# Changing the accumulator layout two blocks ahead of the attention projection, and opening that projection's first two pairs together

## The chip, the cores and the metric

The kernel runs on one core of one Trainium2 chip. The metric is the time of one launch on the device, in microseconds (us); lower is better. The profile shows one execution, engine by engine: TensorE (PE, with its weight loads as PEld), VectorE (DVE), ScalarE (ACT), GpSimd (POOL) and SyncE (SP), the last of which only issues DMAs here.

## The reference

One layer of a decoder, for a prompt of 1024 tokens and 8 single-token samples, 1032 columns in all. Three mixers read the same normalised input; each one's output is projected, multiplied by its gate and summed, and the sum goes through the merge weights:

```python
D_MODEL = 1024; ATTN_HEADS = 4; SSM_D_INNER = 2048; MEM_LEN = 256
sc_b, sc_c, sc_x, z, xbc, dt_raw, q, gates = jnp.split(xn @ w_in, splits, axis=-1)
y_a = (sc_b * conv_u) @ w_sc_out                                  # short convolution
y_b = group_rmsnorm(y_ssd, ssm_norm_w, SSM_GROUPS) @ w_ssm_out    # state-space scan
...                                                               # attention into 256 memory tokens
y_c = attention @ w_attn_o
x = x + (g_a * y_a + g_b * y_b + g_c * y_c) @ w_merge_o
x = x + swiglu(rmsnorm(x))
```

The change touches the end of `y_b`'s projection, all of `y_c`'s, and the sum of the three gated shares. (The last five lines above are shortened from the reference's `mixer_block` and its caller.)

## The kernel before, in words

Activations lie with features on the 128 partitions and the 1032 columns along the free axis. Every f32 matrix product is three products of rounded halves: each operand is split into a high part `h` (a rounding copy on ACT) and a low part `l` (a subtraction on DVE), and PE multiplies high by high, high by low and low by high into one accumulator. A weight block of 1024 rows and 128 columns is loaded by SP into a "raw" tile and split.

PSUM, the accumulators' memory, has 8 banks. Up to the point of the change it is laid out as two accumulators of three banks (`mm_ps`; function `gemm` writes one for each output block, in pieces of 260, 512 and 260 columns, while the other is evicted) and two small ones. Then `mm_stack.close()` drops these, and the pool `pst` lays out three accumulators of two banks, `m0`, `m1`, `m2`, each for half of the columns (`HT` = 516).

The stretch around the change runs as follows.

- `out_part(2, m, ...)` computes the last eight output blocks of `y_b`, in accumulators `po20` to `po27`. For each it loads a gate (`gt`) and the part summed so far (`yr`), adds the accumulator to `yr` on DVE (L1497), multiplies by the gate (L1498), and leaves the store to `yg_d` to be issued during the next block (`owed`). So `yg_d` holds the gated share of `y_b`, and `mg_d` that of `y_a`.
- The attention for the samples runs beside these blocks (`so`, `os_d`, `psob`: their outputs, stored, loaded in another layout and transposed).
- `y_c` is computed with one level of a Strassen-like scheme, by pairs of output blocks: `ao0`, `ao2`, `ao4`, `ao6`. The columns of the activations are split in halves, and sums and differences of their quarters, called forms (`B11`, `B21`, `T1`, `nT2`, `T3`, `B22`, `T4`), are multiplied by a pair's weights (`A`), sums of them (`S`, `T`) or a part of them (`D`): seven products of 24 matmuls, 168 a pair. Each form and each weight combination is split in halves by ACT and DVE. `st_begin` loads and prepares the first pair. `strassen` runs a pair: `B11`, `T1`, `nT2`, `B21`, `T3`, `B22`, `T4`, with evictions on ACT and DVE (L381 subtracts the accumulator of `T3`, L383 that of `B22`) between them.
- In `fetch`, in the middle of each pair, SP loads the gate `gt` and `yg`, and POOL issues a DMA that adds `mg_d` onto `yg`. When the pair is done DVE multiplies by the gate and adds `yg` (L1859 to L1865), which gives two blocks of the sum, the tiles `mg0` to `mg7`.
- These are split (`mgs0h`, `mgs0l`, ...) and multiplied by the merge weights (`wm00` and so on) into accumulators `pm`.

Each engine runs its instructions in the order that a scheduler fixed when the program was built; each of SP's and POOL's DMAs waits in its queue until what it needs is there. Tiles come from pools that rotate (weights three of each kind, `ev` five), so an allocation waits for the last reader of the oldest tile.

Of the kernel before, what the change touches and what calls it, by code (L numbers as in the profile page):

```python
# [17 lines left out]
P = 128  # L18
# [25 lines left out]
def tile_kernel(ctx: ExitStack, tc, a, o):  # L44
# [8 lines left out]

    cp = ctx.enter_context(tc.tile_pool(name="const", bufs=1))
    wp = ctx.enter_context(tc.tile_pool(name="weights", bufs=3))
    ap_ = ctx.enter_context(tc.tile_pool(name="acts", bufs=12))
# [32 lines left out]
    V.memset(ones, 1.0)  # L89
    tri = cp.tile([P, P], F32, tag="tri", name="tri")  # L90
    G.affine_select(
# [107 lines left out]
    def gemm(w, acts, name, width=P, off=0):  # L199
# [19 lines left out]
        return ps  # L219

    def wblock(w, col):
        return w[:, col : col + P].rearrange("(k p) c -> p k c", p=P)
# [7 lines left out]
    freed = [None]  # L230
    count = [0]

# [39 lines left out]
    def st_early(blocks, forms):  # L272


        for first in range(0, len(blocks), 3):
            held = []
            for i, (src1, nm, out, keep) in enumerate(blocks[first : first + 3]):
                wA = st_split(st_raw(src1, f"{nm}Er"), f"{nm}E")
                ps = st_ps(f"m{i}", f"{nm}e")
# [36 lines left out]

    def strassen(src1, src2, forms, nm, sums, outs, early=None, after_t3=None, ready=None, hook=None, add=False, begun=None, mid=None):

# [3 lines left out]
        elif ready is None and early is None:  # L322
            raw1, raw2 = st_raw(src1, f"{nm}r1"), st_raw(src2, f"{nm}r2")
        tags = ("m0", "m1", "m2") if count[0] % 2 == 0 else ("m2", "m1", "m0")
        count[0] += 1
        pa, pb = (st_ps(t, f"{nm}{t}") for t in tags[:2])

# [10 lines left out]
        if early is None:  # L338
            pc = st_ps(tags[2], f"{nm}{tags[2]}")
            if begun is None:  # L340
                wA = st_split(raw1, f"{nm}A")
            prod(pa, wA, 0, "B11", True)
        else:
            tick()
        if ready is not None:
            raw1, raw2, sa, wS, wT = ready
        elif early is not None:
            raw1, raw2, sa, wS = st_sums(src1, src2, nm, sums, freed[0])
        else:
            if begun is None:  # L350
                sa = sums(f"{nm}sa")
                V.tensor_add(sa[:, :512], raw2[:, :512], raw2[:, 512:])
                V.tensor_add(sa[:, 512:], sa[:, :512], raw1[:, :512])
                wS = st_split(sa, f"{nm}S")
            put(o11, pa)
        if ready is None:
# [8 lines left out]
        if early is None:  # L365
            put(o12, pa)
            prod(pc, wA, 512, "B21", True)
            V.tensor_tensor(o11, hv(pc), o11, op=ALU.add)
# [52 lines left out]

    tail_sc = cp.tile([P, 1, 10, 8], F32, tag="tail_sc", name="tail_sc")
    tail_xc = cp.tile([P, 3, 11, 8], F32, tag="tail_xc", name="tail_xc")
    qs = cp.tile([P, 8, NS], F32, tag="qs", name="qs")

# [1048 lines left out]
    def out_part(i, m, w, src, nxt):  # L1474


        nm = f"{i}{m}"
        if m == 0:
            out_in(src)
        if i != 1:  # L1480
            gt = ev_tile(f"gt{nm}")
            SY.dma_start(gt[:, :TT], gt_d[(0, 8, 8)[i] + m])
        if i == 2:
            t = ev_tile(f"yr{nm}")
            SY.dma_start(t[:, :TT], yr_d[m])
        if m == KD - 1 and nxt is not None:
            out_ahead(nxt)
        ps = gemm(weights(wblock(w, m * P), f"wo{nm}"), acts, f"po{nm}")
        if i == 0:
            V.tensor_mul(gt[:, :TT], flat(ps), gt[:, :TT])  # L1490
            owed.append(lambda: SY.dma_start(mg_d[m], gt[:, :TT]))
        elif i == 1:
            t = ev_tile(f"yr{nm}")
            S.copy(t[:, :TT], flat(ps))
            S.dma_start(yr_d[m], t[:, :TT])
        else:
            V.tensor_tensor(t[:, :TT], flat(ps), t[:, :TT], op=ALU.add)  # L1497
# [3 lines left out]
    split = []  # L1501
    outs = deque()
    ins = ((sc_d, a["w_sc_out"][0]), (yb_d, a["w_ssm_out"][0, 0:D]), (yb_d[8:16], a["w_ssm_out"][0, D : 2 * D]), (None, None))
# [72 lines left out]
    if True:  # L1576
# [228 lines left out]
        ats_stack.close()  # L1805
        assert not pend
        while len(outs) > 1:
            run_next(outs)
        for c in (slice(0, T - HT), slice(T - HT, HT)):
# [15 lines left out]
    pst_stack = ExitStack()  # L1825
    pst[0] = pst_stack.enter_context(tc.tile_pool(name="pst", bufs=1, space=PSUM))
    ev_sums = lambda n: ev_tile(n, (P, 1024))
    wa = [wblock(a["w_attn_o"][0], m * P) for m in range(KD)]
    begun = st_begin(wa[0], wa[1], "ao0", ev_sums)
    for kt in range(4):  # L1830
        b12, b22 = raw8[kt][:, HS[1]], raw8[kt + 4][:, HS[1]]
        V.tensor_sub(b12, b22, b12)
        aform("T3", kt, b12)
    for kt in range(4):
        aform("B22", kt, raw8[kt + 4][:, HS[1]])
    for kt in range(4):
        t2, b21 = raw8[kt][:, HS[0]], raw8[kt + 4][:, HS[0]]
        V.scalar_tensor_tensor(t2, t2, -1.0, b21, op0=ALU.mult, op1=ALU.subtract)
        aform("T4", kt, t2)

    merged = []
    for m in range(0, KD, 2):
        oo = [ev_tile(f"ao{m}{i}")[:, :TT] if m == 0 else big(f"mg{m + i}") for i in range(2)]
        gts, ygs = [], []

        def fetch():
            for i in range(2):
                gts.append(ev_tile(f"gt3{m + i}")[:, :TT])
                SY.dma_start(gts[i], gt_d[16 + m + i])
                ygs.append(ev_tile(f"yg{m + i}")[:, :TT])  # L1850
                SY.dma_start(ygs[i], yg_d[m + i])
# [6 lines left out]
        merged += oo if m else [big(f"mg{i}") for i in range(2)]  # L1858
# [3 lines left out]
        V.tensor_mul(oo[1][:, c1], oo[1][:, c1], gts[1][:, c1])  # L1862
        V.tensor_add(merged[m + 1][:, c1], oo[1][:, c1], ygs[1][:, c1])
        V.scalar_tensor_tensor(oo[1][:, c0], pa, -1.0, gts[1][:, c0], op0=ALU.mult, op1=ALU.mult)
        V.tensor_add(merged[m + 1][:, c0], oo[1][:, c0], ygs[1][:, c0])  # L1865
    fxo_stack.close()
# [6 lines left out]
    mg = [split_act(merged[m], f"mgs{m}") for m in range(KD)]  # L1873
    turn_ = deque(("m0", "m1", "m2") if count[0] % 2 else ("m2", "m1", "m0"))

# [40 lines left out]
    for half in range(2):  # L1916
        sq = ev_tile(f"sq{half}")
        for m in range(KD):
# [26 lines left out]
            else:  # L1945
                ps = st_ps(turn_[0], f"pm{half}{m}")
                turn_.rotate(-1)
                merge_part([hv(ps)[:, lo:hi] for lo, hi in HALF], (0, 1))
# [170 lines left out]
    for part, js in enumerate(([0], [9, 10])):  # L2119
# [7 lines left out]

        tags = ("m0", "m1", "m2") if count[0] % 2 == 0 else ("m2", "m1", "m0")
        puts = []
        for m in range(KD):  # L2130
            if not part:
                x2[m] = big(f"x3_{m}")
            for half in range(2):
                ps = st_ps(tags[(2 * m + half) % 3], f"pd{part}{m}{half}")
                for k, (ah, al) in enumerate(hl):
# [10 lines left out]
                else:  # L2146
                    puts.append(S.copy(t, hv(ps)).ins)
        count[0] += 1

        with nullcontext() if part else tc.issue_after(puts[3]):  # L2150
# [178 lines left out]
```

## Time and profile before

| what | value |
|---|---|
| runs, median of 3 | 2444.56 us (2442.44 to 2445.43) |
| profiled execution, its own time | 2446.0 us |
| its span | 2444.3 us |
| mean granted clock of TensorE | 0.996 |
| PE busy | 2394.4 us, 98% |
| DVE, ACT, POOL busy | 67%, 46%, 5% |
| the stretch of the change | about 1529 us (end of `po25`) to 1654 us (first `pm`) |

A row of the timeline reads: start, duration, engine, line, operation, output<-inputs, count, and in brackets the idle time before it and what ended that. The granted clock is the share of full speed that TensorE was allowed.

### The profile page before, as it was taken

Reading aid. Unit: us, or ns where it says so; the run is one execution under the profiler, and the core shown is the slowest. Engines: PE = TensorE matmul, PEld = TensorE weight load, DVE = VectorE, ACT = ScalarE, POOL = GpSimd, SP = SyncE. Lnnn points to the kernel's source line nnn. Section 1 sums busy time; section 2 is a strip of 40 time slices with the busy share of each in tenths; the row PEclk is TensorE's granted clock in tenths of the full one; section 3 lists DMA queues with packets and bytes.
Section 4 is the critical chain, followed back from the end, with each engine's and each line's share of the span. In section 5 each row is a group of like instructions: output and inputs, shape, how many; then the busy total and the mean of one; then the engine's idle time right before and its main releaser. Section 6 shows DMA issues by size and latency. Waiting matters only on the chain.

```text
span 2444.3 us, 45555 instructions
## 1 busy us (share of the span) xinstructions
PE 2394.4 (98%) x18812; PEld 2283.4 (93%) x18812; DVE 1647.5 (67%) x2688; ACT 1112.7 (46%) x1792; POOL 111.5 (5%) x171
## 2 busy tenths in 40 slices
PE   8999999999999999999999999899999999999998
PEld 7999999999999999888888887899999999999998
DVE  6744686777777775568687763764777655567865
ACT  6634555455454544657555442333543333343423
POOL 0000000000000000212211000000000000000000
PEclk9999999999999999999999999999999999999999
DMA  6444423444454346679796887575455332354622
GB/s 213 133 157 155 130 91 111 129 139 130 130 152 118 113 122 194 200 225 296 240 295 213 270 309 271 172 205 182 141 179 163 105 106 95 101 182 149 190 86 80
DMA packets 356678, 407.90 MB, mean 167 GB/s; under 512 B 15230, under 2 KB 276462, under 8 KB 356463
## 3 DMA queue, kind: packets, MB, share of 16 engines
q1 hardware_dynamic: 332182, 337.50, 45.0%
q10 hardware_dynamic: 23137, 63.26, 6.8%
q0 software_dynamic: 1152, 4.23, 0.9%
q8 instruction: 148, 2.42, 0.4%
q14 instruction: 59, 0.48, 0.1%
HBM read 288.81 MB, written 116.35 MB: 166 GB/s over the span
## 4 chain that ended last, share of the span: by engine, by line
PE 84%; DMA 6%; DVE 6%; ACT 1%; issue 1%; SPq 0%; DVEq 0%; ACTq 0%; POOLq 0%; POOL 0%
PE po L218 8%; PE pm L1934 4%; PE ps_q L218 3%; PE py L1063 1%; PE pss L1076 1%; PE ps_z L218 1%; DMA yg<-mg_d 1%; PE po L1055 1%; PE G16m L267 1%; PE d00m L267 1%; PE Z2m L267 1%; PE Z14m L267 1%; PE X18m L267 1%; PE Z10m L267 1%; PE Z6m L267 1%
## 5 line engine op out<-in xcount | busy, mean ns | idle before, releaser
L1007 ACT ACTIVATE r<-r,acum 128x128 f32<-128x128 f32 x256 | 79.3, 391 | 2.9 <-DMA r<-ac_d 2.1
L796 DVE SCALAR_TENSOR_TENSOR ax<-u,prm,ax 128x1024 f32<-128x1024 f32 x44 | 56.3, 1280 | 0.0
L948 ACT ACTIVATE st<-st,es 128x128 f32<-128x128 f32 x128 | 41.3, 392 | 22.4 <-DMA st<-in_state_ssm_dram 22.4
L1040 POOL TENSOR_TENSOR xdd<-xdt,decst 128x512 f32<-128x512 f32 x32 | 35.3, 1102 | 284.3 <-DVE xdt L1036 275.9
L1034 DVE TENSOR_TENSOR r<-r,cbm 128x1024 f32<-128x1024 f32 x32 | 39.1, 1223 | 4.3 <-ACT r L1009 2.4
L1059 DVE TENSOR_TENSOR y<-po,ea 128x512 f32<-128x512 f32 x28 | 19.3, 690 | 31.7 <-PE po L1055 31.7
L950 DVE SCALAR_TENSOR_TENSOR st<-sr,dts,st 128x128 f32<-128x128 f32 x128 | 40.3, 346 | 0.4
L1076 PE MATMUL pss<-xdd,bT 128*128 128x512 f32 x64 | 34.5, 620 | 2.2 <-ACT bT L1033 1.7
L954 DVE SCALAR_TENSOR_TENSOR sr<-st,sr 128x128 f32<-128x128 f32 x128 | 35.4, 286 | 1.1
L1063 PE MATMUL py<-r,xdt 128*64 128x128 f32 x512 | 35.0, 279 | 0.0
L1009 ACT ACTIVATE r<-r 128x1024 f32<-128x1024 f32 x32 | 33.8, 1058 | 0.7
L1949 DVE TENSOR_TENSOR x<-pm,xT 128x516 f32<-128x516 f32 x15 | 10.4, 694 | 34.1 <-PE pm L1934 34.1
L1089 POOL TENSOR_TENSOR s<-s,cdec 128x512 f32<-128x512 f32 x28 | 33.1, 1182 | 0.9 <-DVE s L1082 0.7
L1063 PEld LDWEIGHTS py<-r,xdt 128*64 128x64 f32 x512 | 27.3, 136 | 4.4 <-issue 1.0
L1055 PE MATMUL po<-bc,s 128*128 128x128 f32 x224 | 29.6, 275 | 0.0
L1055 PEld LDWEIGHTS po<-bc,s 128*128 128x128 f32 x224 | 28.0, 191 | 1.0
L1627 ACT ACTIVATE pr<-psa,mx 128x256 f32<-128x256 f32 x32 | 14.9, 471 | 30.2 <-DVE mx L1625 30.2
L799 DVE SCALAR_TENSOR_TENSOR ax<-u,prm,ax 128x1032 f32<-128x1032 f32 x22 | 28.3, 1286 | 0.0
L793 ACT ACTIVATE ax<-u,prm 128x1024 f32<-128x1024 f32 x22 | 27.4, 1246 | 1.7 <-DVE u L383 0.4
L1615 DVE SCALAR_TENSOR_TENSOR kc<-kc,qb 128x256 f32<-128x256 f32 x64 | 23.8, 419 | 5.6 <-DMA qb<-qs_d 5.4
L1036 DVE TENSOR_TENSOR xdt<-xp,dtT 128x512 f32<-128x512 f32 x32 | 21.9, 684 | 8.0 <-PE xp L1029 8.0
L1033 ACT COPY bT<-bp 128x128 f32<-128x128 f32 x32 | 8.4, 262 | 38.5 <-DVE cbm L1031 38.5
(9290 smaller groups left out, 9046.0 us busy)
## 6 DMA issues: line engine op xcount, KB each, us to landing
r<-ac_d SPq DMA_DIRECT2D x32, 512.0 KB
gt_d<-G ACTq DMA_DIRECT2D x24, 516.0 KB
gt<-gt_d SPq DMA_DIRECT2D x24, 516.0 KB
xs_d<-ax ACTq DMA_DIRECT2D x22, 516.0 KB
zs<-zs_d SPq DMA_DIRECT2D x16, 516.0 KB
yb_d<-x SPq DMA_DIRECT2D x16, 516.0 KB
in<-yb_d SPq DMA_DIRECT2D x16, 516.0 KB
st<-in_state_ssm_dram SPq DMA_DIRECT2D x32, 256.0 KB
```

What stands on the lines that cost most here:

```text
L218: PE.matmul(po, wt[:, ks], xc, start=(k == 0 and i == 0), stop=(k == nk - 1 and i == 2))
L267: PE.matmul(po, wt[:, ks], xc, start=(start and kt == 0 and i == 0), stop=(kt == 3 and i == 2), skip_group_check=True,)
L796: V.scalar_tensor_tensor(acc[:, :T], u[:, j : j + T], w[j], acc[:, :T], op0=ALU.mult, op1=ALU.add)
L948: S.activation(st[:, i], st[:, i], AF.Copy, scale=es[:, g * 4 + i, b : b + 1])
L950: V.scalar_tensor_tensor(st[:, i], rb, dts[:, g * 4 + i, b : b + 1], st[:, i], op0=ALU.mult, op1=ALU.add)
L954: V.scalar_tensor_tensor(rb, st[:, i], 1.0, rc, op0=ALU.mult, op1=ALU.mult, accum_out=ys[:, g * 4 + i, b : b + 1],)
L1007: S.activation(r[:, j, :], r[:, j, :], AF.Relu, scale=-1.0, bias=acum[:, c, h : h + 1])
L1034: V.tensor_tensor(r, r, bc(cbm.unsqueeze(1), [P, HPG, P]), op=ALU.mult)
L1055: PE.matmul(po[:, t * P : (t + 1) * P], state["s"][:, t * P : (t + 1) * P], bcg[1][:, cs], start=True, stop=True,)
L1063: PE.matmul(py[hp : hp + 64, (h // 2) * P : (h // 2 + 1) * P], xdt[:, h * 64 : (h + 1) * 64], r[:, (h % 2) * 4 + h // 2, :], start=True, s ...
L1076: PE.matmul(pss, bT, xdd, start=True, stop=True)
L1934: PE.matmul(po, wt[:, ks], x[:, half * HT + lo : half * HT + hi], start=(k == 0 and i == 0), stop=(k == KD - 1 and i == 2),)
```

## The change

The last two output blocks of `y_b` are computed in the new layout by a new function `gemm_halves`: block 26 first for one half of the columns, then for the other, each in an accumulator of two banks; block 27 with both halves side by side. The layout is changed ahead of block 26. The three accumulators rotate by a list, `accs`, in place of the counter `count`.

The projection's first two pairs open together: `st_head` computes `B11` and `B21` of `ao0` and then of `ao2`, before the other products of either; `st_begin` of `ao0` moves ahead of block 27, and the forms of `T3`, `B22` and `T4` are made inside `ao0` (`hook`, `after_t3`). For these two pairs DVE only multiplies by the gate, into the tiles `mg0` to `mg3`, and POOL's DMAs add `yg_d` and `mg_d` onto them, two for each tile. Pairs `ao4` and `ao6` add their shares as before. Some small constants move into a pool (`cx`) that is closed ahead of this, and four gate tiles come from the pool `fxo`.

```diff
+    def gemm_halves(w, acts, name, put, joint):
+        n = int(pace[0] + pace[1])
+        pace[1] += pace[0] - n
+        parts = ((0, 1),) if joint else ((0,), (1,))
...
+        for part in parts:
+            pss = [next_ps(f"{name}{h}") for h in part]
+            for k, (ah, al) in enumerate(acts):
...
+                for i, (wt, x) in enumerate(((w[0], ah), (w[0], al), (w[1], ah))):
+                    for h, ps in zip(part, pss):
+                        for po, xc in halves_of(ps, x, h * HT):
+                            PE.matmul(
...
+            for h, ps in zip(part, pss):
+                put(hv(ps), HS[h])
...
+    def st_head(wA, forms, nm, o11, tags):
+        pa, pc = (st_ps(t, f"{nm}{t}") for t in tags)
+        st_prod(forms, pa, wA, 0, "B11", True)
+        S.copy(o11, hv(pa))
+        st_prod(forms, pc, wA, 512, "B21", True)
+        V.tensor_tensor(o11, hv(pc), o11, op=ALU.add)
+        return pa
+
+    def next_ps(name):
+        ps = st_ps(accs[0], name)
+        accs.rotate(-1)
+        return ps
...
-        ps = gemm(weights(wblock(w, m * P), f"wo{nm}"), acts, f"po{nm}")
+        wm = weights(wblock(w, m * P), f"wo{nm}")
+        if i == 2 and m >= KD - 2:
+            if m == KD - 2:
+                mm_stack.close()
+                pst[0] = pst_stack.enter_context(tc.tile_pool(name="pst", bufs=1, space=PSUM))
+
+            def put(ps, c):
+                V.tensor_tensor(t[:, c], ps, t[:, c], op=ALU.add)
+                V.tensor_mul(t[:, c], t[:, c], gt[:, c])
+
+            gemm_halves(wm, acts, f"po{nm}", put, m == KD - 1)
+            owed.append(lambda: SY.dma_start(yg_d[m], t[:, :TT]))
+            return
+        ps = gemm(wm, acts, f"po{nm}")
...
+        begun = st_begin(wa[0], wa[1], "ao0", ev_sums)
         for c in (slice(0, T - HT), slice(T - HT, HT)):
...
-    mm_stack.close()
...
+    raw_b = st_raw(wa[2], "ao2r1")
+    ta, tb, tc_ = accs
+    heads_ = [st_head(begun[3], aforms, "ao0", oos[0][0][:, HS[0]], (ta, tb))]
+    wA2 = st_split(raw_b, "ao2A")
+    heads_.append(st_head(wA2, aforms, "ao2", oos[1][0][:, HS[0]], (tc_, tb)))
...
+            for i in range(2 if m >= 4 else 0):
                 ygs.append(ev_tile(f"yg{m + i}")[:, :TT])
                 SY.dma_start(ygs[i], yg_d[m + i])
                 G.dma_start(ygs[i], mg_d[m + i], accum_op=ALU.add)
...
-            begun=begun if m == 0 else None, mid=fetch,
+            begun=begun if m < 4 else None, mid=fetch, hook=None if m else form3,
+            after_t3=None if m else last_aforms, head=heads_[m // 2] if m < 4 else None,
...
-        V.tensor_mul(oo[0], oo[0], gts[0])
-        V.tensor_add(merged[m], oo[0], ygs[0])
...
+        V.tensor_mul(merged[m], oo[0], gts[0])
+        V.tensor_mul(merged[m + 1][:, c1], oo[1][:, c1], gts[1][:, c1])
+        if m >= 4:
+            V.tensor_add(merged[m], merged[m], ygs[0])
+            V.tensor_add(merged[m + 1][:, c1], merged[m + 1][:, c1], ygs[1][:, c1])
+        V.scalar_tensor_tensor(merged[m + 1][:, c0], pa, -1.0, gts[1][:, c0], op0=ALU.mult, op1=ALU.mult)
+        if m >= 4:
+            V.tensor_add(merged[m + 1][:, c0], merged[m + 1][:, c0], ygs[1][:, c0])
+        else:
+            for src in (yg_d, mg_d):
+                for i in range(2):
+                    G.dma_start(merged[m + i], src[m + i], accum_op=ALU.add)
```

Three places show what this does to the order of instructions. The first is PE at the end of block 26 (`po_16905` before, `po_16964` its second half after; `ao0m` are accumulators of pair ao0). Before:

```order
10571 L218 MATMUL po_16905<-b07h,wo26l 128x512
10572 L218 MATMUL po_16905<-b07h,wo26l 128x260
10573 L218 MATMUL po_17065<-b00h,wo27h 128x260
10574 L218 MATMUL po_17065<-b00h,wo27h 128x512
10575 L218 MATMUL po_17065<-b00h,wo27h 128x260
```

And now:

```order
10596 L242 MATMUL po_16964<-b07h,wo26l 128x260
10597 L295 MATMUL ao0m_17227<-aB110ah,ao0Ah 128x256
10598 L1744 MATMUL psob<-ident,osr 128x8 x8
10599 L295 MATMUL ao0m_17227<-aB110ah,ao0Ah 128x260
...
10621 L295 MATMUL ao0m_17227<-aB112ah,ao0Al 128x260
10622 L242 MATMUL po_17115<-b00h,wo27h 128x256
```

The 24 matmuls of ao0's `B11` moved ahead of block 27. By the rotation of `accs`, `ao0m_17227` is the accumulator `m1`, which the second half of block 26, `po_16964`, held before it.

The second place is DVE in pair ao2, where L381 of before is L429 now (`ao4r` and `ao4sa`, `ao4sb`, `ao4Al` are the next pair's raw weights, sums and low part). Before:

```order
1603 L352 TENSOR_TENSOR ao4sa<-ao4r_17641 128x512
1604 L353 TENSOR_TENSOR ao4sa<-ao4sa,ao4r_17639 128x512
1605 L255 TENSOR_TENSOR ao2Dl<-ao2r_17420,ao2Dh 128x512
1606 L368 TENSOR_TENSOR mg_17416<-ao2m_17424,mg_17416 128x516
1607 L255 TENSOR_TENSOR ao4Al<-ao4r_17639,ao4Ah 128x1024
1608 L381 TENSOR_TENSOR mg_17417<-mg_17417,ao2m_17422 128x516
```

And now:

```order
1604 L398 TENSOR_TENSOR ao4sa<-ao4r_17690 128x512
1605 L283 TENSOR_TENSOR ao4Al<-ao4r_17688,ao4Ah 128x1024
1606 L399 TENSOR_TENSOR ao4sa<-ao4sa,ao4r_17688 128x512
1607 L327 TENSOR_TENSOR ao4sb<-ao4r_17688,ao4r_17690 128x512
1608 L328 SCALAR_TENSOR_TENSOR ao4sb<-ao4sa,ao4r_17688 128x512
1609 L429 TENSOR_TENSOR mg_17528<-mg_17528,ao2m_17283 128x516
```

Both steps of `ao4sb` moved ahead of the subtraction of `T3`, which stands behind the first use of `ao4r` in either order.

The third place is POOL's queue from the end of the scan on (`mg_17519` and `mg_17520` are mg0 and mg1, `mg_17678` and `mg_17528` mg2 and mg3, `yg_17813` to `yg_18037` yg4 to yg7). Before, it held the eight additions of `mg_d` to yg0 to yg7. Now:

```order
166 L1952 DMA mg_17519<-yg_d 128x1032
167 L1952 DMA mg_17520<-yg_d 128x1032
168 L1952 DMA mg_17519<-mg_d 128x1032
169 L1952 DMA mg_17520<-mg_d 128x1032
170 L1952 DMA mg_17678<-yg_d 128x1032
171 L1952 DMA mg_17528<-yg_d 128x1032
172 L1929 DMA yg_17813<-mg_d 128x1032
173 L1952 DMA mg_17678<-mg_d 128x1032
174 L1952 DMA mg_17528<-mg_d 128x1032
175 L1929 DMA yg_17816<-mg_d 128x1032
176 L1929 DMA yg_18034<-mg_d 128x1032
177 L1929 DMA yg_18037<-mg_d 128x1032
```

The additions onto mg0 to mg3 came in ahead of and between those onto yg4 and yg5. In SP's queue the four loads of yg0 to yg3 are gone, and the load of merge block 1 (`wm01r`) moved from behind the load of yg7 to a place ahead of that of yg6 and its gate.

More of the change, by code (lines that the diff above doesn't have):

```diff
@@ L230, in tile_kernel @@
     freed = [None]
-    count = [0]
+    accs = deque(("m0", "m1", "m2"))
     def b3(t, n):
@@ L315, in st_begin, with strassen @@
         return raw1, raw2, sa, wA, wS
-    def strassen(src1, src2, forms, nm, sums, outs, early=None, after_t3=None, ready=None, hook=None, add=False, begun=None, mid=None):
+    def st_head(wA, forms, nm, o11, tags):
[9 more added lines that the diff above has]
+        return ps
+    def strassen(src1, src2, forms, nm, sums, outs, early=None, after_t3=None, ready=None, hook=None, add=False, begun=None, mid=None, head=None):
         if begun is not None:
@@ L366, in strassen @@
             put(o12, pa)
-            prod(pc, wA, 512, "B21", True)
-            V.tensor_tensor(o11, hv(pc), o11, op=ALU.add)
+            if head is None:
+                prod(pc, wA, 512, "B21", True)
+                V.tensor_tensor(o11, hv(pc), o11, op=ALU.add)
         else:
@@ L1834, in tile_kernel @@
[L1834 to L1839, printed above, removed]
+    oos = [[ev_tile(f"ao0{i}")[:, :TT] for i in range(2)], [ev_tile("ao20")[:, :TT]]]
+    raw_b = st_raw(wa[2], "ao2r1")
+    ta, tb, tc_ = accs
+    heads_ = [st_head(begun[3], aforms, "ao0", oos[0][0][:, HS[0]], (ta, tb))]
@@ L2133, in tile_kernel @@
             for half in range(2):
-                ps = st_ps(tags[(2 * m + half) % 3], f"pd{part}{m}{half}")
+                ps = next_ps(f"pd{part}{m}{half}")
                 for k, (ah, al) in enumerate(hl):
```

91 lines of the change are left out of this document (59 added, 32 removed).

## The prediction

> **What bounds the kernel now.** I read the page first.
>
> ```profile
> PE 2394.4 (98%) x18812; PEld 2283.4 (93%) x18812; DVE 1647.5 (67%) x2688; ACT 1112.7 (46%) x1792; POOL 111.5 (5%) x171
> PE 84%; DMA 6%; DVE 6%; ACT 1%; issue 1%; SPq 0%; DVEq 0%; ACTq 0%; POOLq 0%; POOL 0%
> ```
>
> PE is busy for 98% of the span and carries 84% of the chain that ended last. The change leaves the columns that PE multiplies the same, so it can only move PE's waits. All of its moved instructions lie between output block 26 (the last block but one of the third output product) and the start of the merge product. So I read next the waits of PE in that stretch, 1500 to 1720 us (engine, line and tile waited for, total us, times, longest):
>
> ```profile
> PE ao0m L267 <- ACT ao0Th L254: 5.0, 1, 5.0
> PE ao0m L267 <- DVE anT20al L395: 2.9, 1, 2.9
> PE pm L1934 <- DVE mg L383: 2.5, 1, 2.5
> ...
> PE ao4m L267 <- DVE ao4Sl L255: 1.6, 1, 1.6
> PE pm L1934 <- DVE wm01l L168: 1.4, 1, 1.4
> PE ao4m L267 <- DVE mg L381: 0.9, 1, 0.9
> PE ao4m L267 <- DVE mg L383: 0.8, 1, 0.8
> PE ao6m L267 <- ACT mg L335: 0.7, 1, 0.7
> PE ao6m L267 <- DVE ao6Sl L255: 0.6, 1, 0.6
> ```
>
> They make 16.4 us: 7.9 in front of and inside pair ao0, 4.6 in ao4 and ao6, 3.9 at the merge product. A wait has a second price here, which the table of windows shows (PE busy and matmuls, PEld, DVE, ACT, POOL, then the granted clock, the DMA share and GB/s):
>
> ```profile
> core 0: us, PE busy (x) PEld busy (x) DVE busy (x) ACT busy (x) POOL busy (x), PEclk, DMA share, GB/s
> 1541.50:1573.70 32.20, 24.30 (x179) 22.39 (x177) 29.66 (x63) 16.14 (x38) 0.00 (x0) 0.98 0.47 151
> 1573.70:1579.20 5.50, 5.50 (x25) 5.50 (x26) 2.94 (x4) 1.41 (x2) 1.01 (x1) 0.50 0.99 291
> 1656.00:1662.00 6.00, 5.73 (x30) 5.73 (x31) 6.00 (x7) 2.12 (x2) 0.00 (x0) 0.57 0.54 158
> 1662.00:1704.00 42.00, 42.00 (x356) 42.00 (x355) 17.20 (x22) 11.38 (x15) 0.00 (x0) 1.00 0.56 177
> ```
>
> At clock 1.00 a half-block matmul takes 42.00/356 = 0.118 us. After the 5.0 us wait 25 of them took 5.50 us at clock 0.50: 5.50 - 25 x 0.118 = 2.55 us lost. After the 2.5 and 1.4 us at the merge 30 took 5.73: 2.2 us lost. After the 2.9 us wait the clock stayed at 0.98. So the stretch costs 16.4 + 2.55 + 2.2 = 21.1 us, and that is all there is to win.
>
> **The change part by part.** *A, up to T3 of ao0.* Rows of the timeline (start us, us, engine, line, what, count):
>
> ```profile
> 1528.80 0.64 PE L218 MATMUL po<-b00h,wo26h 128*128 128x260 f32 x3
> 1529.00 1.23 DVE L1497 TENSOR_TENSOR yr<-po,yr 128x1032 f32<-128x1032 f32 x1 [8.58 <-PE po L218]
> 1541.52 1.10 SPq L1675 DMA_DIRECT2D os_d<-so  x4
> 1541.63 0.64 PE L218 MATMUL po<-b00h,wo27h 128*128 128x260 f32 x3
> 1543.05 0.43 SPq L1485 DMA_DIRECT2D yr<-yr_d  x1
> 1549.89 1.23 DVE L1497 TENSOR_TENSOR yr<-po,yr 128x1032 f32<-128x1032 f32 x1
> 1556.81 0.47 PE L267 MATMUL ao0m<-aB110ah,ao0Ah 128*128 128x256 f32 x2 [2.92 <-DVE anT20al L395]
> 1573.70 0.80 PE L267 MATMUL ao0m<-aT30ah,ao0Th 128*128 128x256 f32 x2 [4.98 <-ACT ao0Th L254]
> 1595.55 0.32 SPq L1851 DMA_DIRECT2D yg<-yg_d  x1
> 1596.69 1.05 ACT L254 CAST ao4Ah<-ao4r 128x1024 fp32r<-128x1024 f32 x1
> 1598.40 1.22 DVE L255 TENSOR_TENSOR ao4Al<-ao4r,ao4Ah 128x1024 fp32r<-128x1024 f32 x1
> 1599.99 0.69 DVE L381 TENSOR_TENSOR mg<-mg,ao2m 128x516 f32<-128x516 f32 x1 [0.37 <-PE ao2m L267]
> 1600.21 0.86 POOL L1852 DMA_DIRECT2D yg<-mg_d  x1 [1.81 <-DMA yg<-yg_d]
> ```
>
> Before, block 26 had an accumulator of its own and began beside the eviction of block 25. Now the accumulators change layout in between, so its first matmul waits for that eviction: 1529.00 + 1.23 - 1528.80 = 1.4, with the signal 1.5 us.
>
> Its second half and the head of ao0 now share a tile, and the head stands on PE ahead of block 27. The tile is free when DVE has added block 26 to `yr`, which first has to be loaded. That load is issued at 1543.05, behind the stores of `os_d` that wait for an ACT copy; the change moves neither. Before, nobody waited for it: block 27 had the other accumulator. It landed by 1549.89 at the latest, where DVE used it without idling; a load of the same size took 1600.21 - 1595.55 = 4.7, so 1547.7 at the earliest. Two half evictions follow, at 0.69 us each as the 516-column step L381. PE has been free since 1541.63 + 1.5 = 1543.1. **A new wait of 6.0 to 8.2 us; I take 6.4**, nearer to the low end, since only one other load of that size is ahead in the queue. Behind it on PE stand the head, `psob` and block 27.
>
> This is longer than the 5.0 us that halved the clock, so I add the 2.55. The half rate then hides the next lateness: block 27's weights are split late (as ao4A's, ACT 1.05 and DVE 1.22, together 2.3 us, behind the sums of ao0), and the 24 head matmuls lose about that time anyway. Without the half clock the 2.3 would appear instead. 0.4 for a last half eviction of block 27 and 0.2 for 48 more, shorter matmuls: 1.5 + 6.4 + 2.55 + 0.6 = 11.05.
>
> Against that the 2.92, the 4.98 and its 2.55 go (10.45). The 2.92 goes because ao0's B11 no longer has the last forms ahead of it. The 4.98 goes if DVE's forms are ready: T3 of ao0 now stands 240 matmuls behind the head's start (block 27, ao0's B11, B21, nT2, T1 and ao2's B11, B21), at 1549.5 + 28.3 + 2.55 + 0.4 = 1580.8. DVE had 29.66 us of work in the window that ends at T3; it now resumes at 1548.2 with that and ao2's split (1.22), so it is ready by about 1579. That cover is thin, 1.7 us. **A: +0.6.**
>
> The Trainium skill, page "TensorE: Matmul & The Clock Gate", section "Why this matters for your kernels", asks for no idle gap over about 3 us between bursts of matmuls, which speaks against this part: by it the new wait pays for a slow stretch as the old one did, and the sum is as above.
>
> *B, the waits in ao2, ao4 and ao6.* Rows on ao4's second weight block, then on the shares:
>
> ```profile
> 1587.97 0.69 DVE L300 SCALAR_TENSOR_TENSOR ao2sb<-ao2sa,ao2r 128x512 f32<-128x512 f32 x1
> 1588.73 0.38 SPq L248 DMA_DIRECT2D ao4r<-in_w_attn_o_dram  x1
> 1595.85 0.69 DVE L352 TENSOR_TENSOR ao4sa<-ao4r 128x512 f32<-128x512 f32 x1 [0.33 <-DMA ao4r<-in_w_attn_o_dram]
> 1607.82 0.70 DVE L1863 TENSOR_TENSOR mg<-mg,yg 128x516 f32<-128x516 f32 x1 [6.41 <-DMA yg<-mg_d]
> 1637.52 0.43 SPq L139 DMA_DIRECT2D wm01r<-in_w_merge_o_dram  x1
> 1641.74 0.86 POOL L1852 DMA_DIRECT2D yg<-mg_d  x1 [18.80 <-DVE mgs2l L178]
> 1644.37 0.86 POOL L1852 DMA_DIRECT2D yg<-mg_d  x1 [1.77 <-DMA yg<-yg_d]
> 1652.52 0.70 DVE L1863 TENSOR_TENSOR mg<-mg,yg 128x516 f32<-128x516 f32 x1 [3.76 <-DMA yg<-mg_d]
> ...
> yg<-mg_d POOLq DMA_DIRECT2D x8, 516.0 KB, 7.3
> ```
>
> *ao2's T4.* It needs DVE's subtraction of T3 (L381, now L429). This stood on DVE behind three steps of ao4's weights; now five (`ao4sa` twice, `ao4Al`, `ao4sb` twice). The load that they wait for is issued when the last half of `ao2sb` is done, now behind the final evictions of ao0, at about 1590.7 instead of 1588.73. With 7.1 us as before (1595.85 - 1588.73) it lands at 1597.8; the five steps and the subtraction (5 x 0.69 + 1.22) end at 1602.5. PE is at T4 408 matmuls behind the head's start: 1549.5 + 48.1 + 2.55 + 0.4 = 1600.6, with small gaps 1601. A new wait of 1.5, and more if the load shares the engines with the two accumulations that are now issued before it: 5.1 if half an accumulation's 7.3 comes on top. I take 2.5, nearer to the load as it was measured.
>
> *ao4.* Its 0.8, 1.6 and 0.9 came from DVE standing still for `yg` (the 6.41). DVE adds nothing for the first two pairs any more: gone, with those additions.
>
> *ao6.* POOL's queue will hold in order: `yg` onto mg0, mg1, `mg` onto them, `yg` onto mg2, mg3, `mg` onto yg4, onto mg2, mg3, then onto yg5. From the end of ao2: mg2 issued at +1 us, mg3 at +3.6 (steps of 1644.37 - 1641.74 = 2.6); mg2's second accumulation waits for its first (7.3), mg3's second for +11.8; yg5 goes behind it at about +14.4 and took 1652.52 - 1644.37 = 8.1 here, so +22.5. Two DVE steps later, +23.9, the accumulator of ao6's T1 is free; PE is there after ao4 and ao6's B11, 192 x 0.118 = 22.7. So 1.2, then 1.9 for `ao6Sl` behind a gate product and its own 1.22. I take 3.7 with some crowding; as before (1.3) if transfers are quick, 7 if three accumulations in a row each take 1 us more. Sum 2.5 + 3.7 = 6.2 against 4.6. **B: +1.6.**
>
> *C, the merge product.* Its 2.5 came from yg7's accumulation (1644.37, used at 1652.52 after 3.76 of DVE idle), its 1.4 from the late split of wm01. SP loads wm01r after yg7 now (1637.52), sharing the engines with it; in the changed order it goes ahead of that group, and four loads of SP are gone. I take 1.6 for what is left of 3.9 and no half clock (2.2): 6.1 becomes 1.6. Ends: 0.4 and, nothing won, 6.1. **C: -4.5.**
>
> **Sum.** 0.6 + 1.6 - 4.5 = -2.3 us. The profiled execution was 2446.0 us (span 2444.3), 1.4 above the median of the runs, 2444.56; I take the same difference from the median: **2442.3 us**. About 0.2%, 4.9 us, is what a measurement of this kernel can tell from no change, so this counts as within it.
>
> **The rivals.**
>
> *Transfers keep up* (0.25). For it: DMA share was only 0.54 to 0.56 from 1656 on. Against: 0.99 in the first 5.5 us behind T3. ao2's T4 then waits 1.5, ao6 as before 1.3, the merge 0.4: 0.6 - 1.8 - 5.7 = -6.9, 2437.7.
>
> *POOL's queue is late* (0.17). Where 8 loads and accumulations of shares stood, 12 transfers of POOL in one in-order queue, 8 of them chained in twos on the same tile, end in front of DVE's addition of yg5. If each of the three in a row takes 2 us more than 7.3, ao6's T1 waits about 10 instead of 3.7, and the clock is halved once more: -2.3 + 6.3 + 2.55 = +6.5, 2451.1. It decides from about 7 us of wait at ao6's T1.
>
> *Every gap of some 3 us closes the gate* (0.10). The 2.9 us wait did not halve the clock, 2.5 and 1.4 close together did: so waits of 2.5 and 3.7 may or may not. If both do, 2 x 2.55 more: +2.8, 2447.4. The Trainium skill ("TensorE: Matmul & The Clock Gate", section "What's actually happening") has the clock fall after one free-running window of 3.4 us without work; the trace agrees as far as a shorter gap went either way.
>
> *T3 of ao0 still waits* (0.05): the 1.7 us of cover isn't there and DVE is late by as much as before; the change doesn't do what it says. +5.0 + 2.55: +5.2, 2449.8. *The merge wait stays* (0.05): +4.5, so 2446.8.
>
> **How the numbers follow.** My forecast has 0.38, and spans 2439 to 2445 by the ends of its terms. Faster by over 0.2% (below 2439.7): the first rival and 0.07 of the forecast's low side, 0.32. Slower (above 2449.5): POOL's queue and the waiting T3, 0.22. Within: 0.46. The range leaves out the outer part of the first two rivals: 2435.5 to 2451.
>
> **What would show it.** In the waits of PE: a wait of about 6.4 of `ao0m` for DVE's `yr`, clock 0.50 behind it; no wait for `ao0Th`; about 2.5 at ao2's T4, about 3.7 in ao6, none in ao4; under 2 at `pm`, with a clock of 1.00. I am wrong if the first is under 4 (then faster), or if `ao6m` waits for 8 or more behind `yg5` (then slower).

## The result and the profile after

The changed kernel took 2441.64 us (median of 12 runs, 2439.09 to 2445.08), the kernel before 2444.11 in runs beside it: 2.5 us less. The ratio is 0.999, 95% interval 0.998 to 1.000. The prediction was 2442.3 us, 2.3 us less, and "within 0.2%" as its likeliest class; both hold. A change of nothing is not ruled out: the interval touches 1, and that of a second series (e1 below) includes it. The waits that make up this number came out differently, though, as the changed kernel's waits of PE show (1500 to 1720 us; line, tile waited for, total us, times, longest):

```profile
PE ao0m L295 <- DVE yr L1543: 6.0, 2, 5.7
PE ao2m L295 <- DVE mg L429: 5.6, 1, 5.6
PE ao6m L295 <- DVE ao6Sl L283: 1.6, 1, 1.6
...
PE po L242 <- DVE yr L1558: 1.3, 1, 1.3
PE ao6m L295 <- DVE mg L431: 1.3, 1, 1.3
```

The waits for `ao0Th`, in ao4 and at `pm` are gone in this profile. In their place stand the wait of ao0's head for `yr`, one of 5.6 us at ao2's T4, and two in ao6. The windows behind three of them, with the granted clock as the third number from the end:

```profile
1545.80:1552.60 6.80, 6.80 (x39) 6.55 (x40) 6.38 (x16) 2.91 (x7) 0.00 (x0) 0.60 0.81 282
1604.09:1609.35 5.26, 5.26 (x24) 5.26 (x25) 3.64 (x4) 0.07 (x1) 0.85 (x1) 0.51 1.05 275
1633.69:1640.01 6.32, 4.72 (x25) 4.51 (x25) 6.32 (x7) 1.32 (x2) 0.00 (x0) 0.73 0.64 186
```

With 0.118 us for a matmul at full clock they lost 6.80 - 39 x 0.118 = 2.2, 5.26 - 24 x 0.118 = 2.4 and 4.72 - 25 x 0.118 = 1.8 us. So a second and a third slow stretch came that the forecast had left to a rival.

The timeline shows the head as predicted: the load of `yr` is issued behind four stores of `os_d`, DVE begins with it, and PE resumes.

```profile
1526.89 0.50 PE L242 MATMUL po<-b00h,wo26h 128*128 128x256 f32 x2 [1.32 <-DVE yr L1558]
...
1538.13 1.10 SPq L1737 DMA_DIRECT2D os_d<-so  x4
1539.66 0.43 SPq L1533 DMA_DIRECT2D yr<-yr_d  x1
1544.45 1.29 DVE L1543 TENSOR_TENSOR yr<-po,yr 128x516 f32<-128x516 f32 x2 [13.92 <-issue]
1545.80 0.58 PE L295 MATMUL ao0m<-aB110ah,ao0Ah 128*128 128x256 f32 x1 [5.71 <-DVE yr L1543]
```

And it shows why T4 waits. DVE stands still for 8.4 us in front of `ao4sa`, until ao4's second weight block is there; the subtraction of T3 (L429) is behind it.

```profile
1588.43 0.38 SPq L276 DMA_DIRECT2D ao4r<-in_w_attn_o_dram  x1
1599.80 0.69 DVE L398 TENSOR_TENSOR ao4sa<-ao4r 128x512 f32<-128x512 f32 x1 [8.38 <-DMA ao4r<-in_w_attn_o_dram]
1603.35 0.68 DVE L429 TENSOR_TENSOR mg<-mg,ao2m 128x516 f32<-128x516 f32 x1
1604.09 0.80 PE L295 MATMUL ao2m<-aT40ah,ao2Dh 128*128 128x256 f32 x2 [5.60 <-DVE mg L429]
```

That load took 11.4 us (1599.80 - 1588.43) where its like took 7.1 before. In the list of DMA issues POOL's transfers are longer than the 7.3 of before, too (KB each, median us to landing):

```profile
mg<-yg_d POOLq DMA_DIRECT2D x4, 516.0 KB, 9.5
mg<-mg_d POOLq DMA_DIRECT2D x4, 516.0 KB, 8.5
...
yg<-mg_d POOLq DMA_DIRECT2D x4, 516.0 KB, 8.9
```

One profile of each kernel can't settle 2.5 us, so the experiments below took a second one of both. The table gives, for several of them, the start of a stage in us after the last group of matmuls of block 25 (`wo25l`), read from the timelines. `wm10h` is the first matmul of the second half of the merge product, where every kernel's work is the same again.

| kernel | block 27 | ao0's B11 | ao0's T3 | ao2's T4 | ao4 | ao6 | `wm10h` |
|---|---|---|---|---|---|---|---|
| before | 13.3 | 28.5 | 45.4 | 74.2 | 77.1 | 101.2 | 175.4 |
| before, again | 13.3 | 28.5 | 46.9 | 75.6 | 78.5 | 104.7 | 177.6 |
| changed | 26.9 | 20.9 | 53.2 | 79.2 | 84.4 | 104.4 | 175.3 |
| changed, again | 26.8 | 20.6 | 53.0 | 78.9 | 84.3 | 104.3 | 173.7 |
| f3 | 15.0 | 27.2 | 48.9 | 76.0 | 78.8 | 99.3 | 167.9 |
| f4 | 27.3 | 20.9 | 53.5 | 74.5 | 77.4 | 97.4 | 163.3 |

In the means of two the stretch got 2.0 us shorter (176.5 to 174.5), which is no more than two profiles of one kernel differ by (2.2 and 1.6). The changed kernel is 7 us behind at ao4 and makes it good from there on: ao4 takes 20.0 us instead of 24.1, and ao6 with the merge 70.9 instead of 74.3 (first profiles).

### The profile page after: what moved, and what is told of

It reads as the page before. It is cut to its first block, busy times and chain, and to the rows that moved or that the text cites. A ratio compares the mean times of both kernels' runs of the same rounds, so it can differ in the third digit from the quotient of the medians.

```text
span 2437.8 us, 45645 instructions
## 1 busy us (share of the span) xinstructions
PE 2393.3 (98%) x18860; PEld 2285.6 (94%) x18860; DVE 1644.2 (67%) x2686; ACT 1113.0 (46%) x1792; POOL 116.3 (5%) x175
## 5 line engine op out<-in xcount | busy, mean ns | idle before, releaser
L996 ACT ACTIVATE st<-st,es 128x128 f32<-128x128 f32 x128 | 41.4, 392 | 20.9 <-DMA st<-in_state_ssm_dram 13.5
L1111 PEld LDWEIGHTS py<-r,xdt 128*64 128x64 f32 x512 | 27.3, 136 | 4.4 <-issue 1.0
```

Of the source, the lines that this page charges most:

```text
L996: S.activation(st[:, i], st[:, i], AF.Copy, scale=es[:, g * 4 + i, b : b + 1])
L1111: PE.matmul(py[hp : hp + 64, (h // 2) * P : (h // 2 + 1) * P], xdt[:, h * 64 : (h + 1) * 64], r[:, (h % 2) * 4 + h // 2, :], start=True, s ...
```

## The experiments

Theories: **T**, the transfers of the stretch, with the shares that POOL adds, set its waits; **R**, the order on DVE sets that of T4; **Rot**, the list of accumulators changes the down product, far behind the stretch; and more that are named where they are tested. Ratios are to the kernel before, in runs beside it.

**e1 and f1: both kernels a second time.** No edit.

> The changed kernel once more, for a second profile. Theory T (the transfers of the stretch, with the shares that POOL adds, set its waits): from the last row of block 25 (wo25l) to the first matmul of merge block 10 (wm10h) it took 175.3 us and the kernel before 175.4; the same again within 1.5 us, with 4 to 7 us of wait at ao2's T4 and clock 0.5 behind it. Rival N (the 2.5 us between the medians come from elsewhere): the start of block 26 is again earlier than in the kernel before by about 3 us, and so is the end behind merge block 10. If the drift outside is only chance, it changes by 1 us or more.

> The kernel before once more, for a second profile of it. The time must come out as the same. From the last row of block 25 to merge block 10 it took 175.4 us, from the start of u0e to the end 690.2 us (the changed kernel 175.3 and 673.. to be read as 687.3). Theory T: the first repeats within 2 us. Theory Rot (the list of accumulators also changes the down product's waits, which nobody counted): the second repeats within 1 us, 2 to 3 us above that of every kernel with the list. If it comes out at 688 or less, Rot falls and the difference is chance.

The changed kernel: 2441.40 us, ratio 0.9993 (0.9981 to 1.0005). The kernel before: 2445.79, ratio 1.0008 (0.9996 to 1.0020), the same as itself. The stretch came out as 173.7 and 177.6 us, in the rows of the table: 1.6 and 2.2 us from the first profiles, where T gave 1.5 and 2. The waits at the head and at T4 came back (5.4 and 5.5 us), with a clock of 0.50 behind T4; the lower clock in ao6 did not, and a wait of 1.4 us stood at the merge.

Ahead of the stretch the last group of block 25 began at 1528.3 and 1525.5 us before, and at 1524.9 and 1525.9 in the changed kernel. Over all thirteen profiles it began at 1522.8 to 1528.3 in the four built on the kernel before and at 1522.7 to 1530.5 in the nine built on the changed one, so this drift is chance, and N falls for the part ahead. From `u0e` to the end it was 690.2 and 688.3 us before, 687.3 and 687.6 changed: the 690.2 did not repeat to within 1 us, so Rot is not borne out, though 688.3 lies 0.3 above the bound at which it was to fall outright.

**f2: the list of accumulators alone**, in the kernel before.

```diff
-        tags = ("m0", "m1", "m2") if count[0] % 2 == 0 else ("m2", "m1", "m0")
-        count[0] += 1
+        tags = tuple(accs)
+        accs.reverse()
...
-                ps = st_ps(turn_[0], f"pm{half}{m}")
-                turn_.rotate(-1)
+                ps = next_ps(f"pm{half}{m}")
...
-                ps = st_ps(tags[(2 * m + half) % 3], f"pd{part}{m}{half}")
+                ps = next_ps(f"pd{part}{m}{half}")
```

> The kernel before, with the list of accumulators alone: pairs, merge and down products take them in the rotation of the changed kernel, nothing else is changed. Rot: from u0e to the end 687 to 688.5 us instead of 690.2, and the first merge product takes the accumulator that is free first, so its 2.5 us wait shrinks; 2 to 4 us faster than before, which would be the whole gain. T: nothing within 1.5 us; the wait at the merge stays 2 us or more, since it is yg7 that is late.

2444.38 us, ratio 1.0006 (0.9998 to 1.0015): nothing. From `u0e` to the end this profile has 687.7 us, inside Rot's 687 to 688.5, and the thirteen profiles have 687.3 to 688.5 with the list and 688.3 to 690.2 without it. A little of that may be the list's, but the runs leave it no gain of over 0.5 us. The merge still waits, 2.2 and 1.4 us, now for the split of mg6.

**e2: the last stores of the sample attention on ACT.**

```diff
-                SY.dma_start(os_d[b : b + 1, h * 256 : (h + 1) * 256], t[row : row + 1, :])
+                (S if b == NS - 1 else SY).dma_start(os_d[b : b + 1, h * 256 : (h + 1) * 256], t[row : row + 1, :])
```

> The four stores of the last sample's attention output are issued by ACT instead of SP, so that the loads of gt26 and yr26 no longer stand behind them. T: the 5.7 us wait of ao0's head for yr26 falls to 2 to 3 us (then the load of osr is last, for psob), the clock is not halved, and in its place 2.3 us appear at block 27 for its late split; 0.5 to 3.5 us faster than the changed kernel. Rival (the wait is DVE's order or the accumulator itself, not that load): 5 to 6 us stay and the time is the same.

2437.93 us, ratio 0.9975 (0.9963 to 0.9988). The load of `yr` was issued 4.3 us after the last group of block 25 instead of 14.7, and the head's wait fell from 5.7 to 0.8 us (T: 2 to 3), so that load was its cause. Behind it the timeline of PE shows what the long wait had covered:

```profile
1544.20 0.38 PE L295 MATMUL ao0m<-aB110ah,ao0Ah 128*128 128x256 f32 x1 [0.79 <-DVE yr L1543]
1545.51 0.64 PE L1744 MATMUL psob<-ident,osr 8*128 8x8 f32 x8 [0.93 <-DMA osr<-os_d]
...
1552.40 1.23 PE L242 MATMUL po<-b00h,wo27h 128*128 128x256 f32 x4 [3.33 <-ACT wo27h L169]
```

The late split of block 27's weights costs 3.3 us in the open (T: 2.3), and the clock falls to 0.50 behind that instead, which T did not expect. In this one profile the stretch took 175.4 us and nothing was won; its runs were 6 us faster than the kernel before all the same. The profiled execution, 2443.01 us, was the second longest of the twelve, so how much of the 6 us lies in the stretch it doesn't show.

**e3: ao4's sums behind both subtractions of ao2.**

```diff
-        V.tensor_tensor(o12, o12, hv(pb), op=ALU.subtract)
+        subbed[0] = V.tensor_tensor(o12, o12, hv(pb), op=ALU.subtract).ins
...
-                V.tensor_add(sa[:, :512], raw2[:, :512], raw2[:, 512:])
+                with tc.issue_after(subbed[0]) if nm == "ao4" else nullcontext():
+                    V.tensor_add(sa[:, :512], raw2[:, :512], raw2[:, 512:])
```

> DVE forms the sums of ao4's weights only after both subtractions of pair ao2, so that ao2's T4 need not wait for ao4's second weight load. Rival R (the wait is the order on DVE and nothing is behind it): 5.6 us and the 2.4 us of half clock go, 5 to 8 us faster than the changed kernel. T: the wait at T4 goes, but ao6's T1 comes earlier to the same additions of yg5 and waits 7 to 9 us instead of 2.9; the time moves by less than 2 us.

2440.20 us, ratio 0.9988 (0.9978 to 0.9999). In the waits of PE the 5.6 us at ao2's T4 are gone, and 7.1 stand in their place, at ao4's T4. Two rows of DVE show it (L431 is the subtraction of T3 in this kernel):

```profile
PE ao4m L296 <- DVE mg L431: 7.1, 1, 7.1
...
1619.55 0.69 DVE L400 TENSOR_TENSOR ao6sa<-ao6r 128x512 f32<-128x512 f32 x1 [9.47 <-DMA ao6r<-in_w_attn_o_dram]
1623.82 0.68 DVE L431 TENSOR_TENSOR mg<-mg,ao4m 128x516 f32<-128x516 f32 x1
```

The start of ao4 was 8.0 us earlier (76.4 in the table's measure), that of ao6 2.8 later, and `wm10h` came at 173.2, as in the changed kernel. The wait only moved by one pair: DVE now stands still for ao6's second weight block, ahead of ao4's subtraction. R falls as far as the time goes; T had the time, but expected the wait behind yg5 at ao6's T1, where none is left.

**f4: no additions of shares onto mg0 to mg3.** The eight DMAs are left out, and with them two shares of four blocks.

```diff
-        else:
-            for src in (yg_d, mg_d):
-                for i in range(2):
-                    G.dma_start(merged[m + i], src[m + i], accum_op=ALU.add)
```

> The changed kernel without the eight additions of shares onto mg0 to mg3: two shares of four blocks are left out of the sum. T and D (those transfers make the loads late): the wait at ao2's T4 falls from 5.6 to under 1.5 us with no half clock behind it, that of ao6 from 2.9 to under 1, and the merge has none; 8 to 14 us faster than the changed kernel. Rival R (ao4's second load is issued late, behind the last sums of ao2, and lands late by itself): 4 us or more stay at T4 and the gain is under 5 us.

2427.79 us, ratio 0.9940 (0.9927 to 0.9953): 14 us less than the changed kernel. The load of ao4's second block was issued at the same time and landed 5 us earlier:

```profile
1588.42 0.38 SPq L276 DMA_DIRECT2D ao4r<-in_w_attn_o_dram  x1
1594.83 0.69 DVE L398 TENSOR_TENSOR ao4sa<-ao4r 128x512 f32<-128x512 f32 x1 [3.42 <-DMA ao4r<-in_w_attn_o_dram]
```

6.4 us instead of 11.4; the wait at T4 is 0.64, and none is listed in ao6 or at the merge. So it is those transfers that make T4 and ao6 wait, not a late issue; the order on DVE by itself only chose which product waits (e3). The Trainium skill, page "DMA: Bandwidth & Descriptors", section "Issuing engines are not separate DMA queues", says that transfers issued by SP, ACT and POOL run on the same engines and interleave; these two loads of SP, beside POOL's additions and without them, agree.

**e4: the shares of the first two pairs loaded and added on DVE as before**, in the changed kernel.

```diff
-            for i in range(2 if m >= 4 else 0):
+            for i in range(2):
                 ygs.append(ev_tile(f"yg{m + i}")[:, :TT])
...
-        else:
-            for src in (yg_d, mg_d):
-                for i in range(2):
-                    G.dma_start(merged[m + i], src[m + i], accum_op=ALU.add)
```

> The changed kernel, with the shares of the first two pairs loaded and added on DVE as before: only that part is undone. T: without four more accumulations ao2's T4 waits under 1.5 us and ao6 under 1.5; a wait of about 4 us appears where ao2 goes on and DVE stands still for yg0 or yg1; 3 to 6 us faster than the changed kernel. Rival A (adding the shares by DMA is what gained at ao4 and the merge): the 3.3 us of ao4 and some 4 to 6 us at the merge come back; 2 to 5 us slower than the changed kernel.

2442.52 us, ratio 0.9991 (0.9980 to 1.0002), the same as the changed kernel: the 3 to 6 us of T and the loss of rival A both missed. T was right on the sizes of the waits, T4 1.2, ao6 0.4 and one new wait in ao2. The second row is DVE's first addition of a share:

```profile
PE ao2m L295 <- ACT ao2Sh L282: 4.4, 1, 4.4
...
1590.82 1.23 DVE L1944 TENSOR_TENSOR mg<-mg,yg 128x1032 f32<-128x1032 f32 x1 [0.43 <-DMA yg<-mg_d]
```

T was wrong on the cause of the new one: DVE stood still for yg0 by only 0.4 us. What is late is DVE's own work: the two steps of ao2's sums, at 1579.8 and 1580.5 us in the changed kernel and ahead of ao0's last subtractions, stand here at 1589.7 and 1592.6, behind the gate products, the second also behind this addition. From 1520 to 1720 us the waits sum to 16.0 us against 15.8 in the changed kernel, so they moved and did not shrink.

**g2: the additions by DMA alone**, in the kernel before (the same lines as the change has for the first two pairs).

```diff
+        else:
+            for src in (yg_d, mg_d):
+                for i in range(2):
+                    G.dma_start(merged[m + i], src[m + i], accum_op=ALU.add)
```

> The kernel before, with one part of the change alone: the shares of the first two pairs are added onto mg0 to mg3 by DMA. T: ao4's waits (3.3 to 3.9 us) go and a wait of 5 to 7 us at ao6's first products comes; within 4 us of the kernel before either way. Rival A (that part makes the change's gain): 3 us or more faster, no new wait.

2443.14 us, ratio 0.9997 (0.9988 to 1.0006): nothing, as T had it. ao4's waits went, and ao6's first products wait 2.7 and 1.6 us (less than the 5 to 7 expected), T4 of ao2 1.5.

```profile
PE ao6m L267 <- DVE mg L383: 2.7, 1, 2.7
PE pm L1941 <- DVE mg L383: 2.3, 1, 2.3
PE ao6m L267 <- DVE ao6Sl L255: 1.6, 1, 1.6
PE pm L1941 <- DVE wm01l L168: 1.6, 1, 1.6
PE ao2m L267 <- DVE mg L381: 1.5, 1, 1.5
```

The merge still waits here. In this kernel, in f2 and in both profiles of the kernel before, SP loads wm01r behind yg7, and the waits at the merge sum to 3.6 to 3.9 us; in the nine with it ahead (changed, e1 to e4, f3, f4, g1, g3) to between 0 and 2.7. The four are all built on the kernel before and the nine on the changed one, so these profiles don't part that load from the rest of the change.

**f3: three edits on the changed kernel**, those of e2 and e4 and block 27's weights split ahead of ao0's.

```diff
-        wm = weights(wblock(w, m * P), f"wo{nm}")
+        wm = early_w.pop(nm, None) or weights(wblock(w, m * P), f"wo{nm}")
...
+        early_w["27"] = weights(wblock(ins[2][1], 7 * P), "wo27")
         begun = st_begin(wa[0], wa[1], "ao0", ev_sums)
```

> The changed kernel with three edits: the last stores of the sample attention on ACT, block 27's weights split ahead of ao0's, and the shares of the first two pairs loaded and added on DVE as before. T: no wait above 1.5 us up to ao0's T3 and no half clock there; one wait of 4 to 6 us in ao2; 8 to 12 us faster than before. Rival D (the stretch is bound by its transfers, whatever the order): it ends within 2 us of the others, and the wins at the head come back as waits from ao2 on.

**2436.96 us, ratio 0.9974 (0.9962 to 0.9985): faster than both kernels.** The stretch took 167.9 us, 6 to 7 less than in the two profiles of the changed one. The waits that are left in it:

```profile
PE ao2m L295 <- ACT ao2Sh L282: 4.9, 1, 4.9
...
PE pm L2017 <- DVE mgs6l L180: 1.4, 1, 1.4
PE po L242 <- DVE yr L1558: 1.3, 1, 1.3
PE ao0m L295 <- DVE yr L1543: 1.0, 1, 1.0
PE ao0m L295 <- ACT ao L349: 0.7, 1, 0.7
```

Up to T3 no wait is longer than 1.3, as expected. The clock did fall there, though, which T did not expect: behind the waits of 0.7 and 1.0 us, 37 matmuls took 6.00 us at clock 0.72 (1562.74 to 1568.74 us), 1.6 us lost. With the weights split first, block 27 also stands ahead of the head again (15.0 against 27.2 in the table). Rival D, that the transfers bind whatever the order, falls against both kernels: against the mean of the two profiles of before the stretch lost 8.6 us. The runs show 6 to 7, under T's 8 to 12. They don't show that it takes three edits, for e2 has one of them and the same ratio, 0.9975; that the other two add something rests on one profile of each (167.9 and 175.4 us).

**g1: the two edits at the head, without that of the shares.**

```diff
+                (S if b == NS - 1 else SY).dma_start(os_d[b : b + 1, h * 256 : (h + 1) * 256], t[row : row + 1, :])
...
+        early_w["27"] = weights(wblock(ins[2][1], 7 * P), "wo27")
```

> Of the three edits of f3 the two at the head (last stores on ACT, block 27's weights split first); the shares are added onto mg0 to mg3 by DMA as in the changed kernel. T: pairs start earlier, so the additions are later against them: ao6 waits 7 to 9 us, and of f3's gain under half is left, 1 to 4 us faster than before. Rival H (the head makes the whole gain): the same time as f3, 6 us faster than before.

2440.99 us, ratio 0.9981 (0.9972 to 0.9990): 2.8 us less than before by the medians. The interval overlaps that of f3, so the runs alone don't settle H; the waits speak against it. In its one profile the stretch took 176.4 us. T4 waits 5.4 again, with DVE standing still for 11.2 us until ao4's second weight block is there, and ao2's first products wait 3.0 besides; ao6 waits 1.6, not the 7 to 9 that T expected. So in this profile the head's gain comes back as waits where the additions lie, one pair earlier than T said.

**g3: f3 with ao2's sums written ahead of ao0's gate products.** The five lines under the `if` stood at the start of pair ao2.

```diff
+        if m == 0:
+            raw_d = st_raw(wa[3], "ao2r2")
+            sa2 = ev_sums("ao2sa")
+            V.tensor_add(sa2[:, :512], raw_d[:, :512], raw_d[:, 512:])
+            V.tensor_add(sa2[:, 512:], sa2[:, :512], raw_b[:, :512])
+            begun = raw_b, raw_d, sa2, wA2, st_split(sa2, "ao2S")
```

> f3 with the sums of ao2's weights written ahead of pair ao0's gate products, so that ao2's T1 finds them earlier on DVE. If the 4.9 us wait of f3 is DVE's order alone, it falls to about 1.5 us and the time by another 3 to 6 us. If DVE is simply full there (it had no idle from 1573.6 to 1592 us in f3), the wait falls by 1 us at most and another grows, at T4: the same time as f3 or 1 to 2 us slower.

2439.12 us, ratio 0.9980 (0.9971 to 0.9989). The 4.9 fell to 3.9, as was expected if DVE is full up to ao2's T1. Waits of 2.9 and 2.8 us appeared at ao2's B22 and T4, but not because DVE is full there too: it stood still ahead of each, for the accumulation of a share and for ao4's second weight block.

```profile
1593.24 0.70 DVE L1948 TENSOR_TENSOR mg<-mg,yg 128x516 f32<-128x516 f32 x1 [7.28 <-DMA yg<-mg_d]
...
1603.43 0.69 DVE L398 TENSOR_TENSOR ao4sa<-ao4r 128x512 f32<-128x512 f32 x1 [6.02 <-DMA ao4r<-in_w_attn_o_dram]
```

So up to T1 it is DVE's work that sets the wait, and behind it again a transfer. The stretch took 172.4 us in this profile; the runs don't tell it from f3.

## Why the prediction was right

The number and the class were right; of its three parts one was far off, and the other two made up for it. Terms in us, measured in the first profiles.

| term | predicted | measured |
|---|---|---|
| A: block 26 behind the eviction | 1.5 | 1.3 |
| A: ao0's head behind `yr` | 6.4 | 5.7 |
| A: half clock behind it, hiding block 27's split | 2.55 | 2.2, no wait at block 27 |
| A: last eviction, shorter matmuls | 0.6 | 0.3 for the eviction |
| A: T3 behind its forms | 0 | 0 |
| B: ao2's T4 | 2.5 | 5.6 and 2.4 of half clock |
| B: ao4 | 0 | 0 |
| B: ao6 | 3.7 | 2.9 and 1.8 of lower clock |
| C: merge | 1.6 | 0 |

**A** came out at 9.5 against the 10.45 that went: -0.9 instead of +0.6. Its reasoning held at each step, and e2 shows its finest one: the late split of block 27 was there, 3.3 us instead of 2.3, hidden by the slow head. The cover of T3 was larger than the 1.7 us given: `ao0Tl` was done at 1574.4, T3 began at 1578.1.

**B** came out at 12.7 against 4.6: +8.1 instead of +1.6. The step that failed is the load of ao4's second block: "I take 2.5, nearer to the load as it was measured". Its cause was named (two accumulations issued ahead of it) and the upper end, 5.1, nearly held the 5.6; but the value was taken next to a row measured without that traffic. f4 shows its price: 6.4 us without, 11.4 with. The same step left out the slow clock behind such a wait, 2.4 us; that was the third rival, and both of its stretches came in this profile. ao6's waits by themselves were as small as the chain through POOL's queue had given.

**C** came out at -6.1 instead of -4.5. That wm01r moved ahead goes with shorter waits there in all thirteen profiles; it wasn't tried by itself, so what shortened them is not shown.

In the second profile of the changed kernel the same sums are -1.0, +4.8 and -4.7: T4 cost 5.5 and 2.4 us, ao6 only 1.4 at full clock, and 1.4 was left at the merge. So the failed step repeats, and the slow stretch in ao6 does not.

The first three make +1.1, the rows of the first two profiles -0.1 from block 25 to `wm10h`, the means of two -2.0 and the runs -2.5. What lies between +1.1 and -0.1 is in no row of the waits, and the 2 us between two profiles of one kernel are of the size of one slow stretch more or less. So the agreement of the forecast difference with the measured one to 0.2 us is luck; that it is small is not: it was to be a trade of one set of waits for another, and that is what the trace shows.

Of the rivals, "transfers keep up" was wrong by the DMA share (0.89 from 1600 to 1660 us against 0.74 before), as these windows show, before and after; "POOL's queue is late" had the right cause and the wrong place, T4 of ao2 instead of ao6. The waiting T3 did not come, and the merge wait did not stay (0 and 1.4 us in the two profiles).

```profile
1600.00:1660.00 60.00, 51.42 (x404) 49.94 (x403) 41.24 (x49) 19.71 (x24) 4.29 (x5) 0.95 0.74 197
1600.00:1660.00 60.00, 53.00 (x406) 52.46 (x407) 42.88 (x50) 21.04 (x24) 6.92 (x8) 0.91 0.89 220
```

## What to carry to other kernels

Where a change adds transfers to a busy stretch, don't price the other loads there by their own durations of before: 7.1 us became 11.4, and the upper end of the forecast, 5.1 us of wait, was nearer than the 2.5 that was taken. Before a wait is removed, look at what is late next behind it; here it was 3.3 us of weight split behind 5.7 (e2). Where an edit only moves a wait (e3, e4, g1), ask what it stands behind in its new place: in e3 and g1 it was again a weight load beside the shares' transfers, in e4 the work on DVE. Without the additions of the shares in four of the eight blocks the kernel was 14 us faster (f4).

## What the runs showed of the hardware

The same wait did not always slow the clock. Ahead of ao0 PE waited 2.9 us in both profiles of the kernel before; behind it the clock was 1.00 in one and 0.72 in the other (windows of before, then of before again). In f2 and g2 it was 1.00 behind the same wait.

```profile
1556.81:1562.00 5.19, 5.19 (x41) 5.02 (x42) 5.19 (x10) 2.04 (x4) 0.00 (x0) 1.00 0.47 165
1554.00:1560.00 6.00, 5.97 (x37) 6.00 (x38) 4.96 (x10) 1.30 (x2) 0.00 (x0) 0.72 0.55 173
```

Waits of 3.3 us and longer slowed it in all eighteen cases of the thirteen profiles, from 1520 to 1720 us: the clock was 0.50 to 0.63 in the 6 us behind. Pairs of waits of 0.7 to 2.7 us with a few matmuls between them slowed it in twelve cases of fifteen. The smallest pair, 0.7 and 1.0 us at ao0's head, did so in f3 and g1 (0.72 in each) and not in g3 (1.00).

The Trainium skill, page "TensorE: Matmul & The Clock Gate", section "What's actually happening", has the clock follow how busy PE was in free-running windows of about 3.4 us, so that the moment of a change depends on where in the window the work begins; the two rows agree as far as one wait went either way. That such a window has to be wholly idle they don't bear out: no wait under 3.4 us fills one, and 2.9 us, or 0.7 and 1.0 us together, slowed the clock even so.

For a forecast, a wait of about 3 us here has a price of 0 or 1.6 us (6.00 - 37 x 0.118) by chance, which is two thirds of what this change moved.
